# Two chains for the delta rule's triangle inverses, early rows in three output projections, and three modulation products on VectorE

## The chip, the cores and the metric

The kernel runs on one core of one Trainium2 chip. The metric is the device time of one execution in microseconds (us). Each engine runs its own instructions in the order in which the program was scheduled (TensorE, called PE, for matrix products; VectorE, DVE; ScalarE, ACT; GpSimd, POOL; SyncE, SP, which issues nearly all transfers), and the engines wait for each other by semaphores.

## The reference

Four transformer blocks over 256 positions and 1024 channels, all in float32. Every block has two halves, and each half scales and shifts a normed `x` by rows that come from a conditioning vector (six "modulation" rows to a block, `shift, scale, gate` twice). Cut to what matters:

```python
# blocks 1 and 2 (l = 0, 1)
mod = silu(c) @ w_mod[l] + b_mod[l]          # six rows of 1024
h = rms_norm(x, g) * (1 + sc1) + sh1
z = h @ w_in[l]                              # split to four mixers of 256 channels
y = concat(rms_norm(short_conv(z)), rms_norm(sparse_attention(z)),
           rms_norm(gated_linear_attention(z)), rms_norm(gmlp(z))) @ w_o[l]
x = x + gt1 * rms_norm(y)
h = rms_norm(x, g) * (1 + sc2) + sh2
x = x + gt2 * rms_norm(relu(h @ w_up[l]) ** 2 @ w_down[l])
# block 3: hybrid mixer; block 4: retention; both then a gated feed-forward
gdn:   tri = I + strict_lower(beta * k k^T * decay)   # 4 heads
       u, w = solve(tri, [beta * v, beta * k * exp(g)])
stick: A[t, s] = sigmoid(z_ts) * prod(1 - sigmoid(z_tj))   # 8 heads
x = x + gate * (concat(gdn, stick) @ w_out)
```

## The kernel before

Activations lie transposed: channels on the 128 partitions, the 256 positions along the free axis, so `x` is eight tiles of 128x256. Every large product is made of three matmuls in a faster float32 form: weights and activations are split into a high and a low part (`wh`, `wl`; `hh`, `hl` or `oh`, `ol`) and high*high, low*high and high*low are summed in PSUM (L236). A weight tile of 128x2048 comes by SP into one of four buffers `w`; ACT casts its two halves to `wh` (L214), DVE subtracts to get `wl` (L217), four buffers each (`load_split`, L317).

The stages follow each other: the start (`mods_first` makes the first two modulation rows on PE while 8 MB of their weights stream in), mixer 1 of block 1 (`mixer1`), its output projection (`tiles2`, `post1`), its feed-forward, the same for block 2, then the hybrid mixer (`hybrid`), its output projection (`tiles2`, `post2`), feed-forward, retention, feed-forward. Between two stages stands a hand-over: the sum of squares of the last output, `rstd`, then `norm_mod` makes `h`, `hh`, `hl` for eight channel tiles, and the next stage's first matmuls wait for `hh`.

A scheduler that simulates the engines sets each engine's order from the program order. Within a mixer `weave` (L634) takes one step from each of its generators in turn, and after each round it may take steps of the modulation queue (`mod_step`), as many as `FILL` says per round. A modulation row of mode "p" (`mod`, L473) is eight transfers of 512 KB and on PE two matmuls over 512 columns for each, gathered by a small transfer that POOL issues (L494); one of mode "d" (`mod_rows`, L392) is eight products with a sum on DVE (L398). Of the rows for block 1, the first two are made at the start, then 2, 4 and 3 in "p" and 5 in "d"; all others are "d". Row 2 is read in `post1`, rows 4 and 3 in the `norm_mod` behind it.

`post1` and `post2` set `tailed = 3`: the casts of the next two weight tiles are scheduled behind the last square of the old stage (L327).

`tiles2` (L1590) takes the eight 128-row tiles of an output projection for each of four column chunks in turn; two chunks can be open, since `psA` has two banks. The order of the rows is gmlp, gla, conv, nsa in blocks 1 and 2 and stick, gdn in the hybrid.

In the hybrid, `proj2` makes keys, queries and values of a pair of heads (`k0 q0 v0 k1 q1 v1`), then the stick's `sq sk` twice and the gates. `gdn` builds four triangles (two head pairs, two halves of 128 positions) and then inverts all four together, level by level (`gdn_levels`, L1301): 6 levels by 4 triangles. One step is a product into the single bank `po` (X by L), a mask on DVE (Q), a product into `px` (Q by T), a subtraction and a transpose on DVE. Behind the last level and `v1` come `gdn_side`, the state and the gdn output rows.

## Time and profile before

| | |
|---|---|
| median of 3 runs | 1537.33 us (1529.53 to 1538.15) |
| profiled execution | 1532.73 us |
| its span, first to last instruction | 1530.9 us |
| PE busy | 1445.3 us, 94% |
| DVE busy | 1139.9 us, 74% |
| ACT busy | 808.4 us, 53% |

The views used further down are the page itself (one execution), the table of stretches (busy time of each engine in a stretch that I cut at the hand-overs, with the clock that was granted to PE as a share of full speed), the chain of waits (what ended last, in order of time), the timeline, the groups of instructions, and the list of one tile's instructions. A busy PE counts a matmul from start to modelled end, so neighbours overlap.

### The profile page before, as it was taken

Reading aid. Unit: us, or ns where it says so; the run is one execution under the profiler, and the core shown is the slowest. Engines: PE = TensorE matmul, PEld = TensorE weight load, DVE = VectorE, ACT = ScalarE, POOL = GpSimd, SP = SyncE. Lnnn points to the kernel's source line nnn. Section 1 sums busy time; section 2 is a strip of 40 time slices with the busy share of each in tenths; the row PEclk is TensorE's granted clock in tenths of the full one; section 3 lists DMA queues with packets and bytes.
Section 4 is the critical chain, followed back from the end, with each engine's and each line's share of the span. In section 5 each row is a group of like instructions: output and inputs, shape, how many; then the busy total and the mean of one; then the engine's idle time right before and its main releaser. Section 6 shows DMA issues by size and latency. Waiting matters only on the chain.

```text
span 1530.9 us, 28353 instructions
## 1 busy us (share of the span) xinstructions
PE 1445.3 (94%) x11594; PEld 1377.5 (90%) x11594; DVE 1139.9 (74%) x1966; ACT 808.4 (53%) x1348; POOL 19.4 (1%) x57
## 2 busy tenths in 40 slices
PE   7999799998999799998999988999989999899999
PEld 5986699997987799997998778999989999899999
DVE  4774779886786899987887547788678888577664
ACT  5654466544555555443774246565445555466642
POOL 1000100000000000000000000000000000000000
PEclk9999899999999999998999898999999999999999
DMA  9846679994441479983532016666766776445453
GB/s 367 289 189 233 234 258 349 358 336 167 140 188 56 168 286 356 375 316 132 220 113 109 1 56 234 243 233 234 267 246 244 259 257 240 163 157 189 167 168 107
DMA packets 65783, 333.15 MB, mean 218 GB/s; under 512 B 8146, under 2 KB 9460, under 8 KB 41716
## 3 DMA queue, kind: packets, MB, share of 16 engines
q1 hardware_dynamic: 65268, 331.30, 59.2%
q8 instruction: 91, 1.49, 0.4%
q14 instruction: 40, 0.33, 0.1%
q0 software_dynamic: 384, 0.03, 0.0%
HBM read 330.22 MB, written 1.05 MB: 216 GB/s over the span
## 4 chain that ended last, share of the span: by engine, by line
PE 91%; DVE 4%; ACT 2%; DMA 1%; issue 1%; SPq 0%; POOL 0%; DVEq 0%; ACTq 0%
PE pa L236 79%; PE py L236 5%; PE px L236 4%; DVE wl L217 2%; PE po L236 1%; PE pm L236 1%; ACT wh L214 1%; ACT u L211 0%; DMA ab<-row 0%; PE py L239 0%; DVE h L233 0%; DMA mw<-in_wmod 0%; DMA vec<-in_vec 0%; DVE u L217 0%; DVE t L217 0%
## 5 line engine op out<-in xcount | busy, mean ns | idle before, releaser
L217 DVE TENSOR_TENSOR wl<-w,wh 128x1024 fp32r<-128x1024 f32 (+4 forms) x444 | 512.5, 1161 | 214.6 <-ACT wh L214 213.5
L214 ACT CAST wh<-w 128x1024 fp32r<-128x1024 f32 (+4 forms) x444 | 439.9, 999 | 363.8 <-PE pa L236 338.6
L236 PE MATMUL pa<-hh,wh 128*128 128x256 f32 x1920 | 515.6, 289 | 43.9 <-ACT hh L211 43.9
L236 PE MATMUL pa<-hh,wl 128*128 128x256 f32 x1920 | 511.1, 287 | 0.0
L236 PEld LDWEIGHTS pa<-hh,wh 128*128 128x128 f32 x1920 | 373.0, 194 | 51.6 <-ACT hh L211 46.8
L236 PE MATMUL pa<-hl,wh 128*128 128x256 f32 x1920 | 390.1, 285 | 0.0
L236 PEld LDWEIGHTS pa<-hh,wl 128*128 128x128 f32 x1920 | 373.4, 195 | 2.3 <-issue 2.1
L236 PE MATMUL pa<-oh,wh 128*128 128x256 f32 x1184 | 334.4, 286 | 7.4 <-ACT oh L214 7.4
L236 PE MATMUL pa<-oh,wl 128*128 128x256 f32 x1184 | 332.6, 284 | 0.0
L236 PE MATMUL pa<-ol,wh 128*128 128x256 f32 x1184 | 318.6, 283 | 0.2
L236 PEld LDWEIGHTS pa<-hl,wh 128*128 128x128 f32 x1920 | 301.5, 193 | 1.9 <-issue 1.6
L236 PEld LDWEIGHTS pa<-oh,wh 128*128 128x128 f32 x1184 | 227.7, 192 | 12.3 <-ACT oh L214 9.1
L236 PEld LDWEIGHTS pa<-oh,wl 128*128 128x128 f32 x1184 | 226.9, 192 | 2.6 <-issue 1.3
L236 PEld LDWEIGHTS pa<-ol,wh 128*128 128x128 f32 x1184 | 219.2, 191 | 0.6 <-DVE ol L217 0.6
L398 DVE SCALAR_TENSOR_TENSOR mw<-mw,cond 128x1024 f32<-128x1024 f32 x152 | 182.8, 1219 | 0.0
L236 PE MATMUL pa<-wh,hh 128*128 128x256 f32 (+2 forms) x224 | 66.9, 301 | 6.2 <-ACT hh L211 6.2
L236 PE MATMUL pa<-wh,hl 128*128 128x256 f32 (+2 forms) x224 | 66.1, 302 | 1.2 <-DVE hl L233 1.2
L236 PE MATMUL pa<-wl,hh 128*128 128x256 f32 (+2 forms) x224 | 67.1, 300 | 0.0
L211 ACT ACTIVATE sw<-sw 128x256 f32<-128x256 f32 x132 | 55.0, 417 | 3.7 <-DVE sw L230 1.0
L211 ACT ACTIVATE u<-u 128x512 f32<-128x512 f32 (+3 forms) x78 | 42.6, 555 | 18.6 <-DVE u L230 13.1
L211 ACT ACTIVATE hh<-h,mods 128x256 fp32r<-128x256 f32 x64 | 30.7, 505 | 38.8 <-DVE h L233 33.6
L236 PEld LDWEIGHTS pa<-wh,hh 128*128 128x128 f32 x224 | 43.8, 196 | 7.7 <-ACT hh L211 6.6
(359 smaller groups left out, 1348.0 us busy)
## 6 DMA issues: line engine op xcount, KB each, us to landing
mw<-in_wmod SPq DMA_DIRECT2D x176, 512.0 KB, 5.7
w<-in_fwin SPq DMA_DIRECT2D x44, 1024.0 KB, 4.8
w<-in_wup SPq DMA_DIRECT2D x32, 1024.0 KB, 5.0
w<-in_wdn SPq DMA_DIRECT2D x32, 1024.0 KB, 6.7
w<-in_rwin SPq DMA_DIRECT2D x24, 1024.0 KB, 5.0
w<-in_fwo SPq DMA_DIRECT2D x32, 704.0 KB, 4.1
w<-in_win SPq DMA_DIRECT2D x16, 1024.0 KB, 6.1
w<-in_hwin SPq DMA_DIRECT2D x12, 1024.0 KB, 4.8
```

The lines of the kernel that those rows point to most:

```text
L211: return self.nc.scalar.activation(out=out, in_=in_, func=func, **kw)
L214: return self.nc.scalar.copy(out, in_)
L217: return (e or self.nc.vector).tensor_tensor(out=out, in0=a, in1=b, op=op)
L236: return self.nc.tensor.matmul(out, lhsT=lhsT, rhs=rhs, start=start, stop=stop, skip_group_check=True)
L398: self.nc.vector.scalar_tensor_tensor(out=w, in0=w, scalar=1.0, in1=cond, op0=ALU.mult, op1=ALU.mult, accum_out=m[:, j:j + 1])
```

## The change

It does eight things.

1. `gdn` is cut: `gdn_pair(hp)` builds and inverts the two triangles of one head pair as a generator of its own, two of them in the weave; `gdn` waits for both and goes on as before.
2. The values move behind the stick's projections in `ORDER_HYB`.
3. `tiles2` opens all four column chunks in four banks (two A, M, and X or Y): first four of the eight row tiles of every chunk, then the other four.
4. Modulation rows 2, 4 and 3 of block 1 are made in mode "d"; `FILL` for the first mixer goes from 0.7 to 1.0 step per round; the conditioning row for "d" is made right after `mods_first`.
5. The hold on the casts behind the last square goes. Instead the casts of the second weight tile after a `norm_mod` are scheduled behind the third `hh`.
6. At the start five of eight squares of `x` go to DVE, and `rstd` reads PSUM directly.
7. 24 matmuls of 128x128 are added at the start (`warm`).
8. Small order constraints at the start (`angles`, `silu`).

```diff
+X_ACT = (1, 3, 5)
+WARM = 24
-ORDER1 = (6, 7, 4, 5, 0, 1, 2, 3)
-ORDER_HYB = ("k0", "q0", "v0", "k1", "q1", "v1", "sq0", "sk0", "sq1", "sk1", "gate0", "gate1")
-MODE = {(1, 0): "jjpppd", ...
+FIRST1, FIRST_HYB = (6, 7, 4, 5), (4, 5, 6, 7)
+BANKS1, BANKS_HYB = "AAMX", "AAMY"
+ORDER_HYB = ("k0", "q0", "k1", "q1", "sq0", "sk0", "sq1", "sk1", "v0", "v1", "gate0", "gate1")
+MODE = {(1, 0): "jjdddd", ...
-FILL = (0.7, 0, 0)
+FILL = (1.0, 0, 0)
...
     def load_split(self, ap, nk, n):
         w = self.load(ap, nk * n)
-        self.tailed = max(self.tailed - 1, 0)
+        self.since += 1
...
-            with self.after(self.tail) if self.tailed else nullcontext():
+            with self.after(self.hold_act) if self.since == 2 and self.loads > 2 else nullcontext():
                 self.copy(h[:, :m], w[:, a * n:b * n])
...
     def norm_mod(self, r, scale, shift):
...
-                self.act(hi[:, j], h[:, j], AF.Identity, bias=shift[:, k:k + 1])
+                hh = self.act(hi[:, j], h[:, j], AF.Identity, bias=shift[:, k:k + 1])
+                if k == 2:
+                    self.hold_act = hh
...
+        self.since = 0
...
+    def warm(self):
+        ps = self.M(128)
+        for i in range(WARM):
+            self.mm(ps, self.ones, self.ones, i == 0, i == WARM - 1)
...
-        self.weave(FILL[2], self.proj2(v, hs, R), self.gdn(v, R, out), self.stick(v, R, out))
+        G = {"st": {}, "done": 0}
+        self.weave(FILL[2], self.proj2(v, hs, R), self.gdn(v, R, G, out), self.gdn_pair(0, R, G),
+                   self.gdn_pair(1, R, G), self.stick(v, R, out))
...
+    def gdn_pair(self, hp, R, G):
+        while ("q", hp) not in R:
+            yield
+        gt, st = G["gt"], {}
+        for tt in range(2):
...
+            st[tt] = dict(AT=AT, L=L, T=T, X=X)
+            yield
+        yield from self.gdn_levels(st.values())
+        G["st"].update({(hp, tt): g for tt, g in st.items()})
+        G["done"] += 1
...
     def gdn(self, v, R, G, out):
...
-        yield from self.gdn_levels(st.values())
-        while ("v", 1) not in R:
-            yield
+        while G["done"] < 2 or ("v", 1) not in R:
+            yield
+        st = dict(sorted(G["st"].items()))
         self.gdn_side(gt, R, st)
...
+    def tiles2(self, w, xs, first, banks):
+        rest = [k for k in range(8) if k not in first]
+        ps, ws = [], []
         for c in range(4):
-            ps = self.chunk_a(w[c], 8, 2, xs, order)
-            yield [(2 * c + n, ps[:, n]) for n in range(2)]
+            ws.append(self.load(w[c], 2048))
+            ps.append(getattr(self, banks[c])(2, S))
...
+        for ks in (first, rest):
+            for c in range(4):
+                for k in ks:
+                    (wh, wl), (xh, xl) = half(c, k), xs[k]
...
+                if ks is rest:
+                    yield [(2 * c + n, ps[c][:, n]) for n in range(2)]
...
             for j in range(KD):
-                self.sums(sq, self.x[:, j], KD)
+                if j in X_ACT:
+                    self.sums(sq, self.x[:, j], KD)
+                else:
+                    q = self.U(S, s="sq")
+                    with self.after(self.angles), self.after(self.silu):
+                        self.mul(q, self.x[:, j], self.x[:, j])
+                    self.running(sq, q, KD)
+            self.warm()
             p = self.psum_of(sq)
+            r = self.U(S, s="r2")
+            self.rsqrt(r, p, 1.0 / D)
             sx = self.U(S, s="sx")
             self.copy(sx, p)
-            r = self.U(S, s="r2")
-            self.rsqrt(r, sx, 1.0 / D)
         self.mods_first(self.v1[0])
+        with self.later(LATER):
+            self.rows[1] = self.silu_rows(self.rows_c(self.t["c1"]))
```

## Rows read from the trace of the kernel before

**Rows 1.** The page, part 1: busy us, share of the span, instructions.
```profile
PE 1445.3 (94%) x11594; PEld 1377.5 (90%) x11594; DVE 1139.9 (74%) x1966; ACT 808.4 (53%) x1348; POOL 19.4 (1%) x57
```

**Rows 2.** Table of stretches: from:to, length, engines' busy us, PE clock, DMA share, GB/s.
```profile
0.00:42.00 42.00, 29.71 (x376) 23.56 (x377) 18.62 (x38) 24.26 (x56) 5.03 (x21) 1.00 0.96 371
42.00:169.40 127.40, 125.72 (x953) 102.19 (x954) 85.33 (x184) 67.53 (x143) 4.39 (x10) 1.00 0.64 234
169.40:185.60 16.20, 7.28 (x37) 3.53 (x35) 11.59 (x24) 8.51 (x17) 2.06 (x4) 0.86 0.71 270
384.00:488.50 104.50, 100.96 (x779) 90.00 (x779) 79.39 (x174) 58.15 (x124) 2.59 (x7) 0.97 0.38 137
510.30:522.70 12.40, 4.14 (x18) 2.97 (x17) 10.02 (x19) 8.00 (x15) 0.00 (x0) 0.85 0.49 183
522.70:708.30 185.60, 185.60 (x1537) 185.60 (x1538) 164.85 (x254) 92.85 (x129) 1.06 (x2) 0.99 0.80 294
708.30:727.30 19.00, 11.57 (x52) 9.33 (x51) 17.49 (x46) 10.62 (x22) 0.00 (x0) 0.73 0.43 153
838.50:891.60 53.10, 44.55 (x282) 37.27 (x281) 28.11 (x79) 16.67 (x33) 1.25 (x4) 0.90 0.00 1
914.80:922.70 7.90, 1.55 (x6) 0.65 (x5) 6.30 (x8) 5.88 (x10) 0.00 (x0) 0.72 0.26 78
1329.90:1337.50 7.60, 1.12 (x4) 0.31 (x3) 5.92 (x8) 5.53 (x9) 0.00 (x0) 0.82 0.29 87
```

**Rows 3.** The chain of waits: start us, length us, what (xcount).
```profile
139.51 5.25 DMA mw<-in_wmod
178.55 5.99 DMA ab<-row
185.62 186.81 PE pa L236 x1536
488.49 21.80 PE pa L236 x168
831.38 0.39 PE px L236 x4
862.29 1.64 PE py L236 x8
891.65 23.16 PE pa L236 x168
```

**Rows 4.** The chain of waits from 42 to 170 us: shares by line.
```profile
by line: PE pa L236 60.7%; PE py L236 10.4%; PE pm L236 9.1%; PE px L236 8.8%; DMA mw<-in_wmod 4.1%; PE po L236 3.6%; PE py L239 2.3%; PE px L239 0.5%; ACT sq L211 0.3%; issue 0.3%
```

**Rows 5.** Groups: line engine op, out<-in, xcount | busy, mean ns | idle before.
```profile
L398 DVE SCALAR_TENSOR_TENSOR mw<-mw,cond 128x1024 f32<-128x1024 f32 x152 | 182.8, 1219 | 0.0
```

**Rows 6.** Timeline at a hand-over, 912 to 926 us: start, length, instruction [idle before].
```profile
915.81 1.13 PE L236 MATMUL px<-sq,ones 128*128 128x256 f32 x4 [0.59 <-ACT sq L211]
916.06 3.87 ACT L214 CAST wh<-w 128x1024 fp32r<-128x1024 f32 x4
917.12 4.63 DVE L217 TENSOR_TENSOR wl<-w,wh 128x1024 fp32r<-128x1024 f32 x4 [1.42 <-ACT wh L214]
919.84 0.46 ACT L211 ACTIVATE rstd<-px,eps 128x256 f32<-128x256 f32 x1
921.67 0.88 DVE L233 SCALAR_TENSOR_TENSOR h<-x,modsc,rstd 128x256 f32<-128x256 f32 x2
922.75 0.58 PE L236 MATMUL pa<-hh,wh 128*128 128x256 f32 x1 [5.80 <-ACT hh L211]
```

**Rows 7.** Table of stretches, the first 4.4 us behind hand-overs.
```profile
185.60:190.00 4.40, 4.38 (x20) 4.38 (x21) 4.40 (x12) 1.79 (x4) 0.00 (x0) 0.50 0.25 101
1337.50:1341.90 4.40, 4.39 (x21) 4.39 (x22) 4.40 (x12) 2.49 (x6) 0.00 (x0) 0.54 0.80 330
```

**Rows 8.** Tile Q, hybrid: duration ns min/median/max, first and last start.
```profile
L236 PE MATMUL px<-Q,T x96: 217/275/476, 806.8 to 872.9; 128*128 128x64 f32 x96
```

**Rows 9.** Waits of SP's own queue: total us, times, longest us.
```profile
SPq L406 <- DVE mw L398: 109.6, 95, 3.6
```

More of the change, by code (lines that the diff above doesn't have):

```diff
@@ L131 @@
 FIRST_MODS = ("", "", "GG", "MM", "", "", "GG", "MM", "MN")
-LANES = dict(proj1="", nsa="N", gla="G", gmlp="M", conv3="M", proj2="", gdn="G", stick="N")
+LANES = dict(proj1="", nsa="N", gla="G", gmlp="M", conv3="M", proj2="", gdn="G", gdn_pair="G", stick="N")
 class Prog:
@@ L154, in __init__ @@
         self.plan = None
-        self.pend, self.hold, self.last_wl, self.tail, self.tailed = [], None, None, None, 0
+        self.pend, self.hold, self.last_wl = [], None, None
     def nm(self, s):
@@ L387, in silu_c @@
         self.sigmoid(s, c)
-        self.mul(c, c, s)
+        self.silu = self.mul(c, c, s)
         rep = self.C(KD, 32)
@@ L447, in mods_first @@
         b1 = self.V(KD, s="b1")
-        self.stt(b1, b[:, 8:16], 1.0, g[:, 0:8], ALU.add, ALU.mult)
+        with self.after(self.angles):
+            self.stt(b1, b[:, 8:16], 1.0, g[:, 0:8], ALU.add, ALU.mult)
         quad = self.C(1, s="quad")
@@ L502, in sums @@
         q = self.U(S, s="sq")
-        self.tail = self.act(q, src, AF.Square)
+        self.act(q, src, AF.Square)
         self.running(parts, q, keep)
@@ L1331, in gdn_levels, with gdn @@
             yield
-    def gdn(self, v, R, out):
+    def gdn_pair(self, hp, R, G):
         nc = self.nc
         ident = self.c1("ident")
+        while ("q", hp) not in R:
+            yield
+        gt, st = G["gt"], {}
+        b2 = lambda a: a[:, :, None].to_broadcast([128, 2, 128])
+        kn, qn = R["k", hp], R["q", hp]
+        hh = slice(2 * hp, 2 * hp + 2)
+        for tt in range(2):
+            c = slice(tt * 128, tt * 128 + 128)
+            pr = self.X(2, 128)
+            for h in range(2):
+                self.mm(pr[:, h], gt["G"][:, tt, 2 * hp + h:2 * hp + h + 1].to_broadcast([128, 128]), ident,
+                        h == 0, False)
+            if tt == 1:
+                eg = self.U(2, 128, s="eg", lane="M")
+                self.act(eg, pr, AF.Exp)
+            self.mm(pr, self.identb, self.bc(self.mdec, 2), False, True)
+            dT = self.U(2, 128, s="dT", lane="M")
+            for h in range(2):
+                self.act(dT[:, h], pr[:, h], AF.Exp, bias=gt["nG"][:, tt, 2 * hp + h:2 * hp + h + 1])
+            pd = self.X(2, 128)
+            for h in range(2):
+                self.tr(pd[:, h], dT[:, h])
+            pk = self.X(2, 2, 128)
+            for h in range(2):
+                self.mm(pk[:, 0, h], kn[:, h, c], kn[:, h, c], h == 0, False)
+                self.mm(pk[:, 1, h], kn[:, h, c], qn[:, h, c], False, h == 1)
+            L = self.U(2, 128, s="L")
+            self.mul(L, pk[:, 0], b2(gt["beta"][:, tt, hh]))
+            self.mul(L, L, pd)
+            AT = self.U(2, 128, s="AT", lane="N")
+            self.mul(AT, dT, pk[:, 1])
+            T = self.U(2, 128, s="T")
+            X = self.U(2, 128, s="X")
+            self.mul(T, L, self.bc(self.c2("m0"), 2))
+            self.sub(T, self.bc(ident, 2), T)
+            nc.vector.transpose(out=X.rearrange("p h n -> p (h n)"), in_=T.rearrange("p h n -> p (h n)"))
+            st[tt] = dict(AT=AT, L=L, T=T, X=X)
+            if tt == 1:
+                self.mul(eg, eg, qn[:, :, c])
+                st[tt]["qd"] = eg
+            yield
+        yield from self.gdn_levels(st.values())
+        G["st"].update({(hp, tt): g for tt, g in st.items()})
+        G["done"] += 1
+    def gdn(self, v, R, G, out):
+        nc = self.nc
         while "sv" not in R:
@@ L1586, in post2, with half @@
             return None
-        self.tailed = 3
         return self.rstd(sq, D)
-    def tiles2(self, w, xs, order):
+    def tiles2(self, w, xs, first, banks):
+        cols = [slice(0, 128), slice(128, 256)]
+        rest = [k for k in range(8) if k not in first]
+        ps, ws = [], []
         for c in range(4):
-            ps = self.chunk_a(w[c], 8, 2, xs, order)
-            yield [(2 * c + n, ps[:, n]) for n in range(2)]
+            ws.append(self.load(w[c], 2048))
+            ps.append(getattr(self, banks[c])(2, S))
+        halves = {}
+        def half(c, k):
+            a = k // 4
+            if (c, a) not in halves:
+                h = self.hlp.tile([128, 1024], F32R, name=self.nm("wh"), tag="wh")
+                l = self.hlp.tile([128, 1024], F32R, name=self.nm("wl"), tag="wl")
+                self.copy(h, ws[c][:, a * 1024:a * 1024 + 1024])
+                self.last_wl = self.sub(l, ws[c][:, a * 1024:a * 1024 + 1024], h.bitcast(F32))
+                halves[c, a] = h, l
+            return [t[:, k % 4 * 256:k % 4 * 256 + 256] for t in halves[c, a]]
+        for ks in (first, rest):
+            for c in range(4):
+                for k in ks:
+                    (wh, wl), (xh, xl) = half(c, k), xs[k]
+                    for n in range(2):
+                        self.mm(ps[c][:, n], wh[:, cols[n]], xh, k == first[0] and n == 0, False)
+                        self.mm(ps[c][:, n], wl[:, cols[n]], xh, False, False)
+                    for n in range(2):
+                        self.mm(ps[c][:, n], wh[:, cols[n]], xl, False, k == rest[-1])
+                if ks is rest:
+                    yield [(2 * c + n, ps[c][:, n]) for n in range(2)]
     def tiles1(self, w, nl, nk, xs):
@@ L1654, in run @@
                 self.v1[1]["norm2"] = self.v1[1]["norm"][:, 16:24]
-                self.queue = [self.cond1()] + [self.mods(*a, self.v1[0]) for a in STAGE["mix10"]]
+                self.queue = [self.mods(*a, self.v1[0]) for a in STAGE["mix10"]]
             else:
```

57 lines of the change are left out of this document (6 added, 51 removed).

## The prediction

> **What bounds the kernel now.** I read the page first. PE is busy 94% of the span, DVE 74% and ACT 53% [rows 1], so PE is the bound on average, and what can be won is work taken off PE and time in which PE has nothing to do. The chain of waits gives the price of PE's main work: 1536 matmuls in 186.81 us, 0.1216 us each [rows 3]. The table of stretches shows where PE is not at that rate: six hand-overs between stages (16.2 us, two of about 12 us, of which that of 12.4 stands, and three of 7.5 to 7.9 us, of which the first and the last stand; PE is busy 1.1 to 7.3 us in each), a seventh of 19.0 us with DVE busy 17.49 us of it, the stretch 838.5 to 891.6 us in which the hybrid's last pieces run (282 matmuls in 53.1 us), and the start, where the transfers fill 0.96 of the DMA engines [rows 2].
>
> **The change, part by part.** The sum is made against the profiled execution, 1532.73 us, which is 1.8 us of it outside the span; the median of the runs lies 4.6 us higher.
>
> *Modulation rows on DVE.* The PE matmuls into `pm` go; on the chain they are 9.1% of 42 to 170 us [rows 4], 11.6 us. The wait for a transfer of 5.25 us in front of the output projection [rows 3] goes too, but the projection's operands would not have been there much sooner: I count 2 us. In exchange DVE gets 24 products of 1219 ns [rows 5], 29.3 us, and ends with nothing on PE. DVE was busy 85.3 of 127.4 us in that stretch [rows 2]; with the new products it has 114.6 us of work in a stretch that should shrink to about 113 us. Some of the products can run later (rows 4 and 3 are read only in the `norm_mod` behind the projection), but DVE also splits the weights that PE waits for. In the second block the same mixer without any modulation takes DVE 79.4 of 104.5 us [rows 2], so there is no slack of 29 us under it. Ends: nothing lost (the products all fit into holes) and 29.3 us lost (none does). I take 4 us, nearer to the first end, because a feed-forward that carries such products has DVE busy 164.85 of 185.6 us, 89%, with PE busy throughout [rows 2]. Queue: the mw transfers wait on SP for a buffer that DVE frees, and weight transfers stand behind them; this wait exists already, 95 times, 1.15 us on average, longest 3.6 [rows 9], and is covered by four weight buffers of 5.8 us of PE work each (48 matmuls). Mixer 1: -11.6 - 2 + 4 = -9.6 us.
>
> *The hand-over behind it.* It took 16.2 us against 12.4 and its like [rows 2], and its chain ends in the small gather transfer of 5.99 us [rows 3]. Without that it can fall to the others' length, -4 us; nine late products on DVE (11 us) may take 1 us of it. -3 us.
>
> *Early rows.* Before, 24 of an output projection's 192 matmuls ran before the last mixer came in: 168 stand on the chain, in 21.80 and 23.16 us [rows 3]. Now up to 96 can. In the hybrid that is 72 more, 72 x 0.1216 = 8.8 us, if PE has holes for them. In blocks 1 and 2 only gmlp's two row tiles are early, gla and nsa end together, so 24 more, 2.9 us. What is lost: the four results come 2.9 us apart and no longer 5.8 us, and DVE must sum squares behind them and split weights in half the time. I take -2 us for each mixer (between 0 and -2.9).
>
> *Two chains and values late.* The level steps run from 806.8 to 872.9 us [rows 8], 24 steps at 2.8 us, the last 13 of them after the projections are through at 838.5. With the pair 0 free to begin when its own queries are there and the values out of the way, about eight steps and the stick's second half move under the projections. PE's own work does not shrink: in 838.5 to 891.6 us I price the 282 records at about 38 us (0.39 us for four of 64 columns, 1.64 us for eight of 256 in plain float32 [rows 3]; the others between), so holes and slow clock are 15 us. That is the cap for early rows and chains together; below it, the 3 us that early rows get if the levels end where they do. I take 11 us, since early rows are work without any wait that fits any hole: -11 us.
>
> *Casts at the hand-overs.* The timeline shows the mechanism: the sum of squares is done at 916.94, but ACT holds four casts (3.87 us) in front of `rstd` at 919.84, and DVE four subtractions (4.63 us) in front of `h` at 921.67; PE stood 5.80 us [rows 6]. Now the first tile's two halves can be split while PE is still in the old stage (DVE and ACT have holes there), and the second's come behind the third `hh`. `rstd` could start at 916.94, `h` 1 us later, PE at about 919: -3.8 us at best; the second tile's 2.4 us on DVE come later, when PE has one tile's products to do. -3 us for each of three such hand-overs (7.5 to 7.9 us). Where the update of `x` is on DVE too, eight tiles need 1.7 us each there, and DVE work is only moved: I take -2 us for one of the two of about 12 us, -1 us for the one behind mixer 2, where DVE has the most to do, and -1 us for the 19.0 us [rows 2]. Together -13 us; bounds 0 (if the scheduler puts the casts behind the tail all the same) and -25.
>
> *Start.* Squares shared and `rstd` from PSUM make the first `h` sooner, but the last modulation column still comes with the transfers, which fill 0.96 of the time [rows 2]; one 512 KB transfer may be put in front of them, 1.4 us at 371 GB/s. -1 us, between +1.5 and -3. The 24 warm-up matmuls I cost at nothing: PE waits for transfers and is busy 29.71 of 42 us [rows 2]; without that cover they are 48 records at 0.1 to 0.2 us, 5 to 10 us.
>
> Sum: -9.6 - 3 - 4 - 11 - 13 - 1 = -41.6 us, 1491 us.
>
> **A rule from the Trainium skill.** In the first 4.4 us behind a hand-over the clock reads 0.50 at the first and 0.54 at the last of six such stretches [rows 7]: PE restarts at the 1.2 GHz level, 20 matmuls where 36 would fit. The Trainium skill, "TensorE: Matmul & The Clock Gate", section "Why this matters for your kernels", says that gaps in PE's work send the clock back to half and that it is won back only by work. The trace agrees with it; I do not count on shorter gaps keeping the clock up, and that is a rival below.
>
> **Rivals.**
> *The clock stays up.* If hand-overs of 4 us no longer drop it, each of the six gives back half of 4.4 us, 2.2 us, and a little in the hybrid: 13 to 16 us more, 1476 us. Against it: a wait of 5.80 us before one restart, of which about 2 us would remain, is near what cannot be told from these rows.
> *The chains give nothing.* Both chains still share the one bank `po` and PE's order; if steps stay 2.8 us apart [rows 8] and only move, the hybrid gets 4 us instead of 11: 1498 us.
> *DVE becomes the bound of mixer 1.* If DVE cannot be filled beyond those 89%, its 114.6 us need 129, 15 us more than the 114 left by PE in place of my 4, and the nine late products cost some 7 us more behind it: 1509 us. For it: DVE's work is as long as the stretch. The Trainium skill, "Perfetto Trace Analysis", section "Optimizing Scalar/DVE Operations", advises to take work off DVE where it is saturated; this edit goes the other way, and that rule is this rival.
> *It does not do what it says:* casts and rows are scheduled where they were, and the PE work saved is waited out: 1530 us.
> *Slower.* The modulation transfers hold SP's queue. If DVE lags in mixer 1 by more than the weight buffers cover (four times 5.8 us, 23 us), each of the 24 transfers delays a weight tile; at 3.6 us each [rows 9] that is 86 us, 1491 + 86 = 1577 us; it is slower than before once 2 us of each are uncovered. Against it: 95 such waits are covered now.
>
> **How the numbers follow.** Likeliest 0.52 (1491 us, own range 1478 to 1505); clock 0.11; chains 0.11; DVE 0.15; nothing 0.05; slower 0.06. The range 1468 to 1520 leaves out a third of the clock case, a third of the DVE case (its upper end, up to 29.3 us lost) and the last two, 0.2. About 1% is what a measurement tells from no change; 1% below 1537.33 is 1522. Faster by over 1%: the first three and two thirds of DVE, 0.84; within 1%: 0.10; slower: 0.06.
>
> **What would show it.** Right: no pm matmul and no gather transfer; mixer 1's stretch 8 to 12 us shorter with DVE over 90% busy; the chain's last piece before each `post` near 100 to 144 matmuls, not 168; the first level step of pair 0 long before pair 1's triangles, the last before 865 us on the old scale; two casts, not four, between the last square and `hh`. Wrong: PE waiting for `wl` in mixer 1; ACT or DVE casts still in front of `rstd`; SP waiting on mw for longer than 4 us; an idle PE in front of the out projections as long as before.

## The result and the profile after

The changed kernel took 1517.7 us (median of 4 runs, 1516.35 to 1518.75) against 1536.5 us before (median of 4 runs, 1529.53 to 1538.15); the ratio is 0.9886, 95% interval 0.9853 to 0.9918. It is faster, but by 19 us and not by 46. In the profiled executions the span falls from 1530.9 to 1516.5 us, 14.4 us where the sum had 41.6.

First the page of the kernel after: engines, and two groups of instructions (columns as in [rows 1, 5]). Line numbers of helpers have moved by 4.

```profile
PE 1441.0 (95%) x11546; PEld 1386.4 (91%) x11546; DVE 1164.7 (77%) x2016; ACT 805.0 (53%) x1340; POOL 13.0 (1%) x45
L221 DVE TENSOR_TENSOR wl<-w,wh 128x1024 fp32r<-128x1024 f32 (+4 forms) x444 | 512.8, 1161 | 183.9 <-ACT wh L218 183.0
L402 DVE SCALAR_TENSOR_TENSOR mw<-mw,cond 128x1024 f32<-128x1024 f32 x176 | 212.2, 1219 | 0.0
```

The products are 24 more than in [rows 5], at the same 1219 ns. PE is busy 4.3 us less than in [rows 1], with 48 records fewer: the 96 into `pm` are gone, the 48 of the warm-up are new.

The table of stretches of the kernel after, columns as in [rows 2]: the start, mixer 1 up to its last matmul of the output projection, the hand-over behind it, mixer 2's hand-over, a piece of the hybrid, its output projection, and the hand-over behind that.

```profile
0.00:42.00 42.00, 38.38 (x436) 32.66 (x436) 21.14 (x42) 25.30 (x52) 5.02 (x21) 0.96 0.96 370
42.00:155.70 113.70, 110.06 (x863) 99.16 (x862) 92.84 (x191) 65.14 (x141) 0.14 (x2) 0.98 0.56 213
155.70:182.20 26.50, 7.00 (x19) 5.25 (x18) 25.60 (x61) 4.96 (x13) 0.00 (x0) 0.65 0.93 322
503.10:513.30 10.20, 4.36 (x18) 3.26 (x18) 7.54 (x22) 4.30 (x11) 0.00 (x0) 0.93 0.61 251
748.00:774.60 26.60, 20.50 (x148) 18.09 (x147) 18.50 (x33) 20.52 (x34) 0.00 (x0) 0.94 0.38 143
894.90:909.30 14.40, 14.38 (x96) 14.18 (x96) 7.58 (x14) 4.61 (x9) 0.00 (x0) 0.79 0.08 25
909.30:914.20 4.90, 1.56 (x6) 1.06 (x6) 2.09 (x5) 2.24 (x6) 0.00 (x0) 1.00 0.62 251
```

Mixer 1 is 13.7 us shorter (127.4 in [rows 2]), but its hand-over is 10.3 us longer (16.2), with DVE busy 25.60 of 26.50 us. The hand-over behind the hybrid is 4.9 us and not 7.9. The hybrid's last piece is 96 matmuls in 14.4 us and not 168 in 23.16 [rows 3]; yet it starts later, at 894.87 and not at 891.65 us, though the stage began 9.2 us sooner.

By stage, from the first matmul of a stage to that of the next (us, profiled executions; the forecast is the sum's terms that fall in the stage):

| stage | before | after | change | forecast |
|---|---|---|---|---|
| start, mixer 1, hand-over | 185.6 | 182.3 | -3.4 | -15.6 |
| first feed-forward | 198.4 | 194.1 | -4.3 | -2 |
| mixer 2 | 138.7 | 137.0 | -1.7 | -3 |
| second feed-forward | 194.7 | 194.8 | +0.1 | -1 |
| hybrid | 205.4 | 206.1 | +0.7 | -14 |
| third feed-forward | 200.4 | 195.6 | -4.8 | -3 |
| retention | 214.4 | 212.8 | -1.6 | -3 |
| last feed-forward | 193.4 | 194.0 | +0.6 | 0 |

Two stages, mixer 1 and the hybrid, hold the missing 27 us; the others came out as forecast in their sum (-11.7 against -12), not one by one.

The timeline of the kernel after at the hand-over behind the hybrid answers [rows 6]:

```profile
910.58 1.56 PE L240 MATMUL px<-sq,ones 128*128 128x256 f32 x6 [1.30 <-DVE sq L221]
912.18 0.47 ACT L215 ACTIVATE rstd<-px,eps 128x256 f32<-128x256 f32 x1 [1.54 <-PE px L240]
913.14 0.88 DVE L237 SCALAR_TENSOR_TENSOR h<-x,modsc,rstd 128x256 f32<-128x256 f32 x2 [2.61 <-ACT rstd L215]
914.22 0.39 PE L240 MATMUL pa<-hh,wh 128*128 128x256 f32 x1 [2.08 <-ACT hh L215]
```

`rstd` starts 0.04 us behind the sum and `h` right behind `rstd`'s second step; no cast stands between. PE waits 2.08 us where it waited 5.80. The clock in the first 4.4 us behind it is still low:

```profile
182.25:186.65 4.40, 4.40 (x19) 4.23 (x20) 4.40 (x12) 3.55 (x6) 0.00 (x0) 0.50 0.15 60
914.20:918.60 4.40, 4.38 (x24) 4.38 (x25) 4.40 (x9) 3.85 (x7) 0.00 (x0) 0.61 0.00 0
```

Five of the seven such stretches read 0.50, the others 0.61 and 0.68; [rows 7] had 0.50 and 0.54.

### The profile page after: what moved, and what is told of

It reads as the page before. It is cut to its first block, busy times and chain, and to the rows that moved or that the text cites. A ratio compares the mean times of both kernels' runs of the same rounds, so it can differ in the third digit from the quotient of the medians.

```text
span 1516.5 us, 28199 instructions
## 1 busy us (share of the span) xinstructions
PE 1441.0 (95%) x11546; PEld 1386.4 (91%) x11546; DVE 1164.7 (77%) x2016; ACT 805.0 (53%) x1340; POOL 13.0 (1%) x45
## 4 chain that ended last, share of the span: by engine, by line
PE 88%; DVE 7%; ACT 3%; issue 1%; DMA 1%; POOL 0%; SPq 0%; ACTq 0%; DVEq 0%
PE pa L240 75%; PE px L240 5%; PE py L240 4%; DVE wl L221 2%; PE pm L240 1%; PE po L240 1%; DVE h L237 1%; DVE mw L402 1%; ACT wh L218 1%; DVE t L221 1%; ACT u L215 1%; DVE x L221 1%; ACT rstd L215 0%; DVE sq L221 0%; DVE u L221 0%
## 5 line engine op out<-in xcount | busy, mean ns | idle before, releaser
L221 DVE TENSOR_TENSOR wl<-w,wh 128x1024 fp32r<-128x1024 f32 (+4 forms) x444 | 512.8, 1161 | 183.9 <-ACT wh L218 183.0
L240 PE MATMUL pa<-hl,wh 128*128 128x256 f32 x1920 | 394.6, 288 | 0.3 <-DVE hl L237 0.2
L240 PE MATMUL pa<-oh,wh 128*128 128x256 f32 x1088 | 307.5, 285 | 4.8 <-ACT oh L218 4.8
L240 PE MATMUL pa<-oh,wl 128*128 128x256 f32 x1088 | 306.1, 284 | 0.0
L240 PE MATMUL pa<-ol,wh 128*128 128x256 f32 x1088 | 299.3, 283 | 0.1
L240 PEld LDWEIGHTS pa<-oh,wh 128*128 128x128 f32 x1088 | 208.9, 192 | 7.0 <-ACT oh L218 6.4
L402 DVE SCALAR_TENSOR_TENSOR mw<-mw,cond 128x1024 f32<-128x1024 f32 x176 | 212.2, 1219 | 0.0
L240 PEld LDWEIGHTS pa<-oh,wl 128*128 128x128 f32 x1088 | 208.4, 192 | 0.2 <-issue 0.2
L240 PEld LDWEIGHTS pa<-ol,wh 128*128 128x128 f32 x1088 | 204.6, 192 | 0.4 <-DVE ol L221 0.3
L215 ACT ACTIVATE u<-u 128x512 f32<-128x512 f32 (+3 forms) x78 | 42.8, 556 | 10.3 <-DVE u L234 7.6
```

The lines of the kernel that those rows point to most:

```text
L215: return self.nc.scalar.activation(out=out, in_=in_, func=func, **kw)
L221: return (e or self.nc.vector).tensor_tensor(out=out, in0=a, in1=b, op=op)
L240: return self.nc.tensor.matmul(out, lhsT=lhsT, rhs=rhs, start=start, stop=stop, skip_group_check=True)
L402: self.nc.vector.scalar_tensor_tensor(out=w, in0=w, scalar=1.0, in1=cond, op0=ALU.mult, op1=ALU.mult, accum_out=m[:, j:j + 1])
```

## Experiments

Medians are of 4 runs (10 for e14); before was 1534.95 to 1537.10 us in these sessions. "Next stage" is the start of the first feed-forward's first matmul, "hybrid" the length of that stage, both from the profiled execution (before: 185.62 and 205.4; changed: 182.25 and 206.1). "By chunks" is one column chunk of an output projection after another, as before the change.

| run | edit | us | ratio's interval | next stage | hybrid |
|---|---|---|---|---|---|
| e1 | changed, 2.5 modulation steps a round | 1513.7 | 0.9835-0.9867 | 179.6 | 204.4 |
| e2 | changed, three rows on PE, 0.7 steps a round | 1524.6 | 0.9903-0.9943 | 192.8 | 202.7 |
| e3 | changed, one chain | 1521.4 | 0.9882-0.9916 | 182.8 | 210.5 |
| e4 | changed, values early | 1504.8 | 0.9782-0.9811 | 183.1 | 194.9 |
| e5 | e4, 2.5 steps a round | 1501.5 | 0.9762-0.9798 | 179.4 | 192.5 |
| e6 | e4, one chain | 1511.0 | 0.9818-0.9860 | 183.1 | 200.0 |
| e7 | e4, hybrid's projection by chunks | 1507.9 | 0.9802-0.9836 | 182.2 | 196.3 |
| e8 | e4, mixers' projections by chunks | 1507.8 | 0.9795-0.9840 | 180.8 | 199.9 |
| e9 | e4, rest of the steps before the projection | 1505.1 | 0.9785-0.9821 | 183.7 | 193.1 |
| e10 | e9, 0.7 steps a round | 1514.0 | 0.9831-0.9881 | 181.6 | 202.8 |
| e11 | e4, casts not held | 1519.0 | 0.9877-0.9909 | 185.6 | 202.6 |
| e12 | e4, three rows left out | 1493.3 | 0.9709-0.9761 | 171.7 | 194.9 |
| e13 | e4, transfers whole, products of 64 columns | 1499.0 | 0.9747-0.9803 | 176.3 | 194.8 |
| e14 | before, rows on DVE alone | 1536.2 | 0.9992-1.0022 | 186.0 | 207.1 |
| e15 | e4, old condition rows, 2 warm-ups | 1505.5 | 0.9788-0.9841 | 183.9 | 193.6 |
| e16 | e8, 2.5 steps a round | 1508.8 | 0.9793-0.9851 | 179.4 | 201.3 |
| e17 | e8, three rows on PE, 0.7 steps a round | 1503.6 | 0.9760-0.9817 | 181.9 | 194.1 |
| e18 | e8, one row on PE, two on DVE, 1.5 steps a round, rest before the projection | 1508.3 | 0.9790-0.9862 | 177.9 | 200.9 |

### The hybrid: order, chains, early rows

```diff
-ORDER_HYB = ("k0", "q0", "k1", "q1", "sq0", "sk0", "sq1", "sk1", "v0", "v1", "gate0", "gate1")
+ORDER_HYB = ("k0", "q0", "v0", "k1", "q1", "v1", "sq0", "sk0", "sq1", "sk1", "gate0", "gate1")   # e4
```

> The changed kernel with the hybrid's projections in the old order (values right behind the keys and queries of their pair); two chains and early rows as changed. Theory (four convolved chunks in a row with the first pair's triangles beside them make ACT and DVE late: PE had holes of 1.67 and 4.43 us and only 28 matmuls from 770 to 780 us): the holes shrink to the 4.5 us of the kernel before, total 1512 to 1515 us. Rival (the order is what lets the first chain begin early): the last level step comes later by 3 to 8 us and the total is 1520 to 1525 us.

Measured 1504.8 us, 13 us faster than the changed kernel. My theory had the size far too small, and the waits that it named are only a part, as the next lines show; the rival is out: the level steps end sooner, not later. The tile `Q` of the changed kernel, then of e4:

```profile
L240 PE MATMUL px<-Q,T x96: 217/275/323, 798.4 to 876.6; 128*128 128x64 f32 x96
```

```profile
L240 PE MATMUL px<-Q,T x96: 217/275/323, 779.2 to 860.4; 128*128 128x64 f32 x96
748.00:774.60 26.60, 24.93 (x206) 24.24 (x205) 23.91 (x49) 21.08 (x37) 0.00 (x0) 1.00 0.42 137
```

The second line is e4's table of the stretch that stands above for the changed kernel: PE gets 206 matmuls done there and not 148, DVE is busy 23.91 us and not 18.50. Four convolved chunks in a row, each with its norm, make PE wait 4.43 us for one norm in the changed kernel; e4 has no such wait:

```profile
772.71 2.07 PE L240 MATMUL px<-u,ones 128*128 128x512 f32 x2 [4.43 <-ACT u L215]
```

But e2, with the same order, waits there for no more than 1.67 us at a time and its hybrid is still 202.7 us long. What all three kernels with the new order and two chains share (changed, e1, e2) is a late first level step, 87.1 to 90.3 us after the stage's first matmul, where all those with the old order have it at 69.4 to 76.5. The first level step needs both triangles of the first pair, and the program asks for the second one a round behind the first: in the new order that round begins with `k1 q1`, two convolutions with their norms, in the old one with `v0`, one without a norm. DVE builds that triangle (`L<-px,be`) at 785.71 us in the changed kernel and at 772.81 in e4.

The 11.2 us are one pair of kernels. The hybrid of the old order took 192.5 to 202.8 us from kernel to kernel (last section), that of the new one 202.7 to 206.1. So the later first step is shown and the size of what it costs is not: it lies anywhere between nothing and 13.6 us, and near 11 only where the old order gets its shorter form.

One chain again, with the new order (e3) and with the old (e6):

```diff
-        yield from self.gdn_levels(st.values())      # in gdn_pair
+        yield from self.gdn_levels(st.values())      # in gdn, over all four
```

> The changed kernel with the triangles of both pairs of heads inverted in one chain of four again, begun when both pairs are ready; the order of the projections and the early rows as changed. By the forecast two chains and late values were worth 8 us together with the rows, so one chain should cost 4 to 8 us: 1522 to 1526 us. Theory after the result (the 24 steps still follow each other through one bank, and a chain of two triangles only makes each step less full): no cost or a gain of up to 5 us, 1512 to 1518 us, with the last level step at or before 876 us.

> The changed kernel with the old order of the hybrid's projections and with one chain of four triangles: what is left of the hybrid's edit is the early rows. Theory (with the old order the two chains are worth what the forecast put on them, the first pair's level steps go under the projections): 5 to 9 us slower than two chains in that order, 1510 to 1514 us, with the last level step 10 us or more later than 860 us. Rival (the gain of the run before came from the order alone and chains do nothing, since all steps go through one bank): 1505 us.

e3: 1521.4 us, just below the forecast's range, hybrid 4.4 us longer; the theory that chains do nothing falls. e6: 1511.0 us, as its theory had it, hybrid 200.0 and not 194.9, with the first `px<-Q,T` at 800.8 and the last at 864.4 us: 4 us later, not the 10 that the theory named. e3 is 4.4 to 7.8 us longer than the three two-chain kernels in its order. e6 has no wait of 3.27 us, and is 5.1 to 7.5 us longer than the seven two-chain kernels without it (last section). So two chains are worth some 4 to 8 us in either order, from one kernel each.

e7 puts the hybrid's output projection back to one chunk after another.

> The changed kernel with the old order of the hybrid's projections, and with the hybrid's output projection back to one chunk after another, so that 24 of its 192 matmuls can run before the delta rule's results and not 96. Theory (early rows fill holes of the level steps): 5 to 9 us slower than with them, 1510 to 1514 us, with a last piece of 168 matmuls near 20 us. Rival (the holes are filled by nothing else but also do not move the end, because the results are what sets it): 1505 to 1507 us.

1507.9 us, hybrid 1.4 us longer: below the theory's 5 to 9, at the edge of the rival. By chunks the projection's last part takes 19.0 us and not 12.8, but it starts at 881.10 and not at 885.80 us. In e4 DVE splits no weights between 829 and 885.78 us; it is on PE that 18 early matmuls into `py` (from 879.03 us) stand in front of the sum that the last delta rows' norm needs:

```profile
881.28 1.02 PE L240 MATMUL px<-u,ones 128*128 128x512 f32 x2
```

### Rows on DVE

The edit by itself on the kernel before:

```diff
-MODE = {(1, 0): "jjpppd", ...
+MODE = {(1, 0): "jjdddd", ...
...
-FILL = (0.7, 0, 0)
+FILL = (1.0, 0, 0)
```

> The kernel before with one edit alone: block 1's first rows on DVE, one step a round. The forecast priced it at -9.6 us in the mixer and -3 us behind it. By the forecast: 1523 to 1525 us and the feed-forward at 173 us. Theory after the runs (what PE gains DVE takes back behind the mixer): the feed-forward begins between 180 and 186 us, total 1530 to 1537 us. Rival (it is the early rows that spoil the hand-over, and without them the products fit): 176 us or sooner.

1536.2 us, ratio 1.0007: nothing, as the theory had it. The table of stretches of e14, cut at the end of the last matmul of the output projection, shows both sides, against 127.40 and 16.20 us in [rows 2]:

```profile
42.00:158.20 116.20, 111.08 (x874) 98.98 (x874) 95.72 (x200) 65.73 (x142) 0.13 (x2) 1.00 0.59 218
158.20:185.95 27.75, 6.08 (x19) 4.25 (x18) 25.90 (x55) 8.03 (x16) 0.00 (x0) 0.68 0.85 310
```

The mixer gains 11.2 us, the hand-over gives 11.5 back. Why, SP's own part of the timeline in the changed kernel shows:

```profile
100.80 1.47 SPq L410 DMA_DIRECT2D mw<-in_wmod  x2
143.71 3.73 SPq L281 DMA_DIRECT2D w<-in_wup  x4
148.26 3.76 SPq L410 DMA_DIRECT2D mw<-in_wmod  x4
155.98 0.33 SPq L281 DMA_DIRECT2D w<-in_wup  x1
```

From 102 to 143.7 us SP issues nothing: next in its queue are the next stage's weights, whose buffers the output projection holds, and 12 of the 24 modulation transfers stand behind them. The other 12 were issued by 102 us, yet four of their products too come only from 147.0 us on, behind the splits in DVE's order: 16 of the 24 products are late, 12 of them with late transfers. In e14 the last of the projection's splits starts at 149.6 us and the first of the 16 late products at 150.7. In the changed kernel they run from 147.0 us, the last 12 between the steps of the hand-over (158.9 to 179.7 us). The timeline at its end:

```profile
178.53 1.22 DVE L402 SCALAR_TENSOR_TENSOR mw<-mw,cond 128x1024 f32<-128x1024 f32 x1
179.68 1.22 DVE L402 SCALAR_TENSOR_TENSOR mw<-mw,cond 128x1024 f32<-128x1024 f32 x1
181.50 0.16 DVE L221 TENSOR_TENSOR mods<-mod,vec 128x8 f32<-128x8 f32 x1
181.69 0.91 ACT L215 ACTIVATE hh<-h,mods 128x256 fp32r<-128x256 f32 x2 [8.99 <-DVE mods L221]
182.25 0.58 PE L240 MATMUL pa<-hh,wh 128*128 128x256 f32 x1 [14.01 <-ACT hh L215]
```

The first `h` was there at 177.55; `hh` waits for the last row's products. Four runs tried whether the products fit sooner: e1 (more steps a round), e9 (what is left drawn before the projection), e10, and e8 (no held buffers).

> The changed kernel with one number altered: 2.5 instead of 1.0 modulation steps drawn per round of mixer 1, so that 21 of the 24 products stand ahead of the output projection's work in DVE's order instead of 8. Theory (the products are late only because the program issues them late; DVE was idle for 21 of the 113.7 us from 42 to 155.7 us): the 26.5 us from the last early matmul of the mixer (155.7) to the first matmul of the feed-forward (182.3) fall to about 16, the mixer's own part grows by at most 3 us; total 1508 to 1511 us. Rival (DVE is the bound of mixer 1 and has no room): the mixer's part grows by as much as the hand-over gives back, total 1515 to 1520 us, with PE waiting for the splits of weights.

> The changed kernel with the old order of the hybrid's projections; modulation steps drawn at the changed kernel's rate of 1 a round, but what is left after mixer 1 is drawn before the output projection's weights are asked for, so that the other 16 products stand between the mixer's last pieces in DVE's order. Theory (DVE is full from 60 to 120 us and has 11 us of holes from 120 to 156; products belong there): hand-over 155.7 to 182.3 shrinks to about 14 us, the mixer ends 2 to 6 us later, first matmul of the feed-forward at 174 to 178 us, total 1497 to 1501 us. Rival (any product ahead of the projection costs PE its own length, as with 2.5 steps a round): feed-forward at 180 us, total 1501 to 1504 us.

> As the run with the steps drawn before the output projection, at the old rate of 0.7 steps a round in the mixer: 5 products go from the full stretch to the stretch behind it. Theory (the full stretch is where a product costs most): the feed-forward begins up to 3 us sooner than at rate 1. Rival (it is the sum over the mixer that counts): the same within 1 us.

> The changed kernel with the old order of the hybrid's projections, and with the output projections of both mixers back to one chunk after another; modulation rows and steps as changed. Theory (early rows hold all four weight buffers, SP's queue stops at the next stage's weights from 102 to 143.7 us and the modulation transfers behind them come late): the hand-over behind mixer 1 shrinks from 26.5 to 18 us or less though the program issues the products where it did, the mixer ends at most 4 us later, mixer 2 is unchanged; total 1498 to 1502 us. Rival (products are late by their place in the program): hand-over still 24 us or more, total 1505 to 1509 us.

e1: the hand-over shrinks to 13.5 us as the theory had it, but the mixer ends 10.3 us later, as the rival had it; 2.7 us are left, and the total lies between the two. e9: feed-forward at 183.7 us, even later than the rival's 180. e10: 181.6, 2 us sooner than e9, as its theory had it; its total is long by the hybrid (last section). e8: hand-over 23 us, far from the theory's 18 and near the rival's 24, next stage 2.3 us sooner than in e4; SP still asks for the next stage's weights first (four, from 111.03 to 150.34 us; the modulation transfers from 151.49), so the main cause is the place in the program, and not that early rows hold the buffers. Where the products stand early DVE is full (tables of e9 and of e5, which has e1's edit):

```profile
100.00:140.00 40.00, 29.77 (x186) 25.30 (x185) 39.36 (x87) 12.55 (x26) 0.00 (x0) 0.83 0.62 211
```

```profile
84.00:121.90 37.90, 31.20 (x245) 27.14 (x243) 37.73 (x79) 15.08 (x32) 0.00 (x0) 0.96 0.78 286
```

How much the rows cost, and which half of them:

```diff
+            if (blk, l) == (1, 0) and i in (2, 3, 4):      # e12: the bias, doubled; no transfer, no product
...
+            ... in0=w[:, :n], scalar=1.0, in1=cond[:, :n], ...     # e13: n = 64, whole transfer
```

> The changed kernel with the old order of the hybrid's projections, with the modulation rows 2, 3 and 4 of block 1's first layer left out (their bias is put in place): no transfers and no products for them. The run shows what all 24 products cost in mixer 1 and behind it, where the feed-forward began at 183.1 us. Theory (DVE is the bound, products cost PE a good part of their 29 us): mixer and hand-over are as long as in the second mixer, 137 us, less the 60 matmuls that PE does ahead of the first stage (7 us), so that the feed-forward begins at about 174 us or sooner and the total is 1494 to 1497 us. Rival (products are hidden and something else sets the hand-over): 180 to 183 us, total 1501 us or more.

> As the run without the rows, but with their transfers, and with products of 64 columns instead of 1024 (the rest of the sums is left out), so that SP's queue and the DMA engines do what they did and DVE nearly nothing. Theory (DVE's time is what the rows cost): within 2 us of the run without the rows. Rival (late transfers behind the next stage's weights are what the hand-over waits for): within 2 us of the kernel with whole products, feed-forward at 181 us or later.

Without them the next stage begins at 171.7 us, 11.4 us sooner than in e4, as e12's theory had it (the total lies 0.7 us below its range); with their transfers and products of 0.22 us at 176.3. Neither of e13's theories holds alone: the transfers, with what is left of the products, cost 4.6 us, the rest of the products 6.8. In e13's timeline DVE waits for the last transfers, and PE for DVE:

```profile
174.05 0.23 DVE L402 SCALAR_TENSOR_TENSOR mw<-mw,cond 128x64 f32<-128x64 f32 x1 [1.36 <-DMA mw<-in_wmod]
175.29 0.22 DVE L402 SCALAR_TENSOR_TENSOR mw<-mw,cond 128x64 f32<-128x64 f32 x1 [1.01 <-DMA mw<-in_wmod]
176.32 0.58 PE L240 MATMUL pa<-hh,wh 128*128 128x256 f32 x1 [15.62 <-ACT hh L215]
```

Rows back on PE, in the changed kernel (e2) and with the mixers' projections by chunks (e17), and one of three (e18):

> The changed kernel with three of block 1's first rows back as matmuls on PE, at the old rate of 0.7 steps a round; everything else as changed. The forecast priced this edit at -9.6 us in the mixer and -3 us behind it, so undoing it should cost about 12.6 us by the forecast: about 1530 us. Theory after the result (the mixer itself gained 13.7 us but 10 of them came back behind it): undoing it costs only 3 to 5 us, 1521 to 1523 us, and the hand-over to the first feed-forward is short again, 16 us or less, on a mixer that ends 10 us later. Rival (the edit has no part in it): 1517 us.

> The changed kernel with the hybrid's projections in the old order, the mixers' output projections one chunk after another, and the three rows as matmuls on PE at 0.7 steps a round: mixer 1 is that of the kernel before with the new start and the new casts. Theory (rows on DVE give nothing, as in the run with that edit alone): the feed-forward begins at 181 to 184 us, total 1503 to 1507 us, as with products on DVE drawn at 1 a round (1507.8 us). Forecast (the rows are worth 12.6 us on DVE): 1516 us or more.

> As the last two, with two of the three rows on DVE and one on PE, all drawn before the output projection. Theory (16 products fit the holes of DVE and 8 steps on PE those of PE): the feed-forward begins at 174 to 178 us, total 1495 to 1500 us. Rival (each engine is full already in the part where the steps must stand): 179 to 183 us, total 1501 us or more.

e2 alone would have spoken for the forecast: 10.6 us later at the next stage (its total, 1524.6 us, lies between the theory's 1523 and the forecast's 1530). But there the early rows' third chunk takes the bank that the rows' matmuls need, and 16 steps of four matmuls stand behind the projection (from 163.8 to 187.6 us). Without early rows (e17) PE's rows reach the next stage at 181.9, as soon as DVE's in e4 and e8 (183.1, 180.8). The mixture (e18) reaches it first of all kernels with whole rows, at 177.9 us, as its theory had it (e5 and e16: 179.4); its total missed the theory's 1495 to 1500 us, with a hybrid of 200.9 us (last section).

### Early rows in the mixers, casts, start

In mixer 2, which no products disturb, the stage took 135.8 to 137.0 us with early rows (the changed kernel and the runs made from it with early rows, but for e11, whose casts differ) and 134.5 to 136.0 us by chunks (e8, e16, e17, e18): they gain nothing and may cost 1 us. In mixer 1, e8 (e4 by chunks) starts the next stage 2.3 us sooner, e16 (e5 by chunks) at the same 179.4 us.

> The changed kernel with three edits: the hybrid's projections in the old order, the mixers' output projections one chunk after another, and 2.5 modulation steps a round. Theory (early rows were worth nothing in the mixers, and their weight splits crowd DVE): the feed-forward begins at 177 to 179 us, total 1498 to 1501 us. Rival (no difference to the run with early rows and 2.5 steps a round, 1501.5 us): 1501 to 1504 us.

1508.8: the theory's 177 to 179 was just missed; both totals are out, with a hybrid of 201.3 us (last section). Pieces of the chain of waits of the changed kernel in mixer 2's last tiles show what stands in for PE:

```profile
496.17 1.07 ACT wh L218
497.27 1.23 DVE wl L221
498.50 0.67 DVE sq L221 x2
500.51 1.14 DVE wl L221
502.65 0.67 DVE xt L221 x2
506.15 2.84 PE px L240 x12
```

In [rows 3] PE's 168 matmuls were one piece up to 510.29 us; now the second halves' splits and the squares, crowded behind them, carry the chain.

> The changed kernel with the old order of the hybrid's projections and without the order that puts the second weight tile's cast behind the third `hh` at the hand-overs; the kernel before had held the casts in another way, this has none. By the forecast the edit of the casts is worth 3 us at a hand-over of the second block and 1 to 2 us elsewhere, 13 us in all, so taking the order away should cost 8 to 13 us over the 1504.8 us of that kernel: 1513 to 1518 us, with PE idle 5 to 8 us in front of `hh` instead of 2.1 or 4.4. Rival (the gain came from having two casts pulled into the old stage, not from holding the third and fourth): the same within 3 us.

e11 (the `after(self.hold_act)` left out): 1519.0 us, 14 more than e4. 7.8 of these are the hybrid, whose order changed (below); the other stages lost 6.5. The idle in front of `hh` stayed at 2.07 and 4.38 us, except behind mixer 1, so that part of the expectation is wrong: what grew is the wait in front of the last sum of squares, 3.12 us and not 1.64 behind the hybrid, 11.24 and not 5.54 behind mixer 1. The last two hand-overs, from the last matmul of the old stage to the first of the next, are 4.1 us in e11, 3.8 in e4 and 7.6 before: most of the gain there came with the end of the old hold. Behind the mixers and the hybrid e11's are 2.8 to 4.6 us longer than e4's: there the new hold keeps casts away from the squares.

> The changed kernel with the old order of the hybrid's projections, the rows of the condition fetched and worked on in mixer 1 again and not at the start, and 2 warm-up matmuls instead of 24. Theory (the new transfer of 512 KB in front of the others costs what its bytes take, 1.4 us): mixer 1 begins 1 to 2 us sooner than 45.3 us. Rival (what came at 2 us is another thing: the squares and the first `h` on DVE): no change there. The total is expected within 3 us of 1504.8 us either way, since the rows' products wait for the condition.

e15: PE goes on with mixer 1 at 41.80 us and not at e4's 45.26 (changed kernel 43.98, before 42.00), so the new transfer or the warm-up, taken out together, did cost it, more than the theory's 1 to 2 us; but the feed-forward starts at 183.9 us all the same. The start's 2 us are swallowed behind mixer 1.

### Together

> Two edits to the changed kernel at once: 2.5 modulation steps a round in mixer 1, and the hybrid's projections in the old order. Alone they gave 1513.7 and 1504.8 us against 1517.7. Theory (they act in different stages and add up): 1500 to 1502 us. Rival (what one gives another stage takes back): 1504 to 1507 us.

e5 gave 1501.5 us, as added up: the fastest whole kernel here, ratio to before 0.9780 (0.9762 to 0.9798).

## Why the prediction was wrong

**Rows on DVE.** The term for the mixer was right: -9.6 forecast, -11.2 by itself (e14). The step that failed is the next: "nine late products on DVE (11 us) may take 1 us", -3 us in all. Sixteen came behind the last split, 19.5 us of DVE, most of them between the steps of the hand-over where nothing covers them, and the transfers of twelve came late too: +11.5 us. I had looked for room on DVE and on SP, but not for where in the program the 16 steps are asked for: behind the output projection, hence behind its last split and the next stage's weights. And the room was smaller than the 25 of 29.3 us that I let fit into holes: with 21 and not 8 of the products drawn early (e1), 15.8 us of DVE, the mixer ended 10.3 us later, and with DVE 98 to 100% busy PE waits. The rival "DVE becomes the bound of mixer 1" was the nearer one in size; it put the end 18 us above the forecast, and this stage came out 12.2 above it. Its mechanism came only in its second half, the products behind the mixer: the mixer itself shrank, with DVE busy 82% of it. The Trainium skill's rule cited with it ("Perfetto Trace Analysis", section "Optimizing Scalar/DVE Operations") is borne out in part: DVE stood at 39.36 of 40 us in e9, and the kernel without the work was 11.4 us sooner, but the work moved to PE brought nothing (e17, 181.9 us against 180.8 in e8). The rival "slower" named the two kinds of transfers in one queue, but the wrong way round: the weights held up the modulation.

**Hybrid.** -11 us were put on chains, early rows and "the values out of the way". The step that failed is the last of these: about eight level steps were to move under the projections, and one did. The first came 90.3 us after the stage's first matmul, 89.4 before, and the stage was 0.7 us longer. I had also misread where the projections end: their last matmul starts at 827.9 us and not at 838.5, so that 5 of the 24 steps stood in front of it before, 6 in the changed kernel (831.9 us) and 8 in e4 (825.4). In the old order chains gave 5.2 us and early rows 1.4, in one pair of kernels each, and with the shorter hand-over the stage was 10.5 us shorter (e4, 194.9) of the 14 forecast; the new order took 11.2 back. I priced the order as a help, by counting level steps, and never asked what ACT and DVE have to do when four chunks with convolution and norm follow each other. It had no rival either. The rival "chains give nothing" is out, as far as one kernel in each order shows it.

**Early rows in the mixers.** -2 us each, nothing or about +1 measured in mixer 2, 0 to +2.3 in mixer 1. "DVE must sum squares behind them and split weights in half the time" stood there as a reservation; the chain of waits in mixer 2 speaks for it.

**Casts.** Right, and a little small. From the last matmul of the old stage to the first of the next, the six hand-overs were to lose 2, 1 and 1 us and three times 3 us; they lost 4.4, 2.1, 1.9, 3.0, 3.8 and 3.8. Some of it was lost again in the rest of a stage: retention is 1.6 us shorter and not 3.8, the second feed-forward not at all. Why is open. The "seventh of 19.0 us" was misread: the hybrid's first matmul starts at 717.37 us, so the hand-over was 9.1 us and the rest was the hybrid.

**Start.** -1 us forecast, +2.0 measured (43.98 against 42.00 us), outside the bound of +1.5; no effect behind mixer 1.

**Clock.** The rival "the clock stays up" did not come in the changed kernel: 0.50 behind the three waits of 4.4 us and the one of 14 us; behind the three of 2.08 us it is 0.61, 0.50 and 0.68. The Trainium skill's rule on the gate ("TensorE: Matmul & The Clock Gate", section "Why this matters for your kernels") agrees with the longer waits. But e4 shows the rival, behind the same waits of 2.07 us:

```profile
903.87:908.27 4.40, 3.48 (x24) 3.06 (x25) 4.40 (x9) 3.85 (x7) 0.00 (x0) 1.00 0.00 0
1310.29:1314.69 4.40, 3.47 (x24) 3.06 (x25) 4.40 (x9) 3.85 (x7) 0.00 (x0) 1.00 0.00 0
```

In the changed kernel and the runs made from it, the clock stayed at 1.00, the 2.4 GHz level, behind 11 of the 54 waits of 2.1 us and behind none of the longer ones. It was worth little there: 24 matmuls in the 4.4 us, as many as at 0.61 above, with DVE busy for all of it. Behind the one of these waits with 0.50 in the changed kernel (1109.80 us) it is 20. Four matmuls at 0.1216 us make 0.5 us (an estimate), not the 2.2 that the rival gave each hand-over.

Of the list of signs: the gather is gone and, behind the hybrid, no cast stands between the last square and `rstd`; the mixer shrank by more than 8 to 12 us but with DVE at 82% and not over 90%; the last piece of the hybrid's projection was 96 matmuls; the first level step did not come long before the second pair's triangles but behind the first of them (795.12 us); the last came at 876.6 us, which is 885.8 on the old scale, not before 865. Of the signs of being wrong, SP waited for a buffer of the modulation for up to 4.3 us.

## What to carry to other kernels

Work moved off the bounding engine is worth what is left when it is followed to the place where its result is read: ask when its transfers get into their queue and what stands ahead of them, not only whether the other engine has idle time. A new order of projections is priced by the engines behind each of them, not by PE. And try every part of a bundle by itself: here one edit (the order, 11.2 us) hid more than two others gave (6.6).

## What was not expected

An edit in one stage changed another stage's order. The hybrid's code is the same (but for e11's casts) in e4, e5, e9, e12, e13, e15 and e17 (192.5 to 194.9 us) and in e8, e10, e11, e16 and e18 (199.9 to 202.8 us); what differs is the order that its instructions were given when the program was scheduled. Timelines of DVE, e17 first, then e16:

```profile
764.61 2.46 DVE L237 SCALAR_TENSOR_TENSOR cv<-zc,vec,cv 128x255 f32<-128x255 f32 x6 [0.15 <-ACT cv L215]
766.98 1.22 DVE L221 TENSOR_TENSOR wl<-w,wh 128x1024 fp32r<-128x1024 f32 x1
769.20 0.42 DVE L221 TENSOR_TENSOR L<-px,be 128x256 f32<-128x256 f32 x1 [0.66 <-PE px L240]
```

```profile
765.24 0.42 DVE L221 TENSOR_TENSOR L<-px,be 128x256 f32<-128x256 f32 x1 [0.58 <-PE px L240]
766.12 0.47 DVE L237 SCALAR_TENSOR_TENSOR cv<-zc,vec,cv 128x255 f32<-128x255 f32 x1
766.83 0.87 DVE L237 SCALAR_TENSOR_TENSOR cv<-zc,vec,cv 128x255 f32<-128x255 f32 x2
```

In e17 the six steps of the convolution go first and the triangle behind them; in e16 the triangle is threaded between them, and PE then waits 3.27 us for the norm. All five of the longer ones have that wait and none of the others. The wait itself is less than half of the difference; the first level step comes 73.3 to 76.5 us after the stage's first matmul in the five, 69.4 to 70.4 in the seven. That the order alone makes the rest is not shown. So kernels that differ outside the hybrid were compared by stage, differences in the hybrid of less than 10 us between single kernels tell little, and whether e18's mixer with e5's hybrid would be faster than 1501.5 us was not tried.
